# A two-layer hybrid attention step: first weights loaded earlier, squares moved to ScalarE, the softmax scale folded into the query copies

## Chip, cores and metric

The program runs on one core of one Trainium2 chip. The metric is the device time of one execution in microseconds. Before the change it is 833.89 us, the median of three runs (833.1 to 834.7).

## What is computed

Two trunk layers act on 512 latent and 128 context tokens (640 columns) of width 1024, in fp32. A layer computes

```python
mod = silu(cond) @ ada_w + ada_b             # shift, scale, gate: 3 x 1024, for c and for c_ctx
h = rmsnorm(x, norm_g) * (1 + scale) + shift
parts = h @ w_in                             # width 3872, cut into ten parts
# A: latent attention, 4 heads, softmax(q k / sqrt(96)) v
# B: gated convolution of width 3
# C: differential attention, 4 heads: softmax(q0 k0 / 8) - lam * softmax(q1 k1 / 8), times v, then a norm
x = x + gate * ((concat(A, B, C) * silu(z)) @ w_out)
```

Latent queries see the latent keys and 128 cached context keys, context queries only the 128 context keys. Outputs are the final norm of x and the context states.

## The kernel before

Activations lie transposed: 128 channels on the partitions, 640 tokens along the free dimension, eight such tiles `hs[kt]` for the 1024 channels. Everything is handled in two halves `j` of 320 tokens. TensorE works in a split form: each fp32 operand becomes a rounded high part (a cast on ScalarE, L324, L390) and a low rest (a subtraction on VectorE, L326, L394; GpSimd does it for some weights), and a product is three matmuls (L362 to L364). Weights come in 15 units per layer of 256 or 272 columns, each in two halves of four `kt`, loaded on the SP queue (L319).

**The start.** The modulation of layer 0 needs `silu(cond) @ ada_w` for shift and scale. That is four blocks `cc` of eight 256 KB loads: blocks 2 and 3 make the scale, 0 and 1 the shift, each for one half of the channels. Block 0 is summed on VectorE (L448, L450), the others by fp32 matmuls on TensorE (L462), two instructions per load. A block's result goes through a copy on ScalarE (L465) and four small transposes (L468) into `mod`. SP's order is: blocks 2, 0, the first token half of x, block 3, the eight loads of block 1, unit `qk0`, the second token half of x, unit `dv0`. In program order eight block-1 products stand before the first projection `p0qk` (L969). The second half's squares for the norm run on GpSimd (L238) and are summed on VectorE (L245).

**The layer.** `main()` is a generator that yields after a few matmuls; `units()` yields one attention unit at a time (4 diff heads of 5 units, then 4 latent heads of 5). `adv` (L1043) mixes them: each advance runs one piece of `main`, steps the background pieces (weight casts, rotary, norms), and at fixed advance numbers (`SIDE0`, `C1`, `C2`, `SIDES`, L1050) one step of `side()`. A side step loads one 256 KB tile of the remaining modulation weights (L148) and reduces it twice on VectorE (L153). Layer 0 has 48 side steps, layer 1 has 16, for the gate that the output projection multiplies with (L1164). Counting the yields, a layer has 228 advances; layer 1 does its 16 steps at advances 24 to 92.

**A diff unit** (L599) makes two score tiles of 128x640 in PSUM (two buffers, shared with the transposes of the weights E). For each VectorE takes the row maximum (L624), then both are multiplied by the negative scale (L625), ScalarE takes the exponent with that bias and accumulates the sum (L631), VectorE makes the ratio (L633, L634) and combines both maps (L636). A latent unit does the same for one map (L886, L887, L889).

The instructions are put in order per engine by a scheduler at build time; an engine then works through its list in order. `pin` keeps an instruction behind what was traced before it on its engine.

Of the kernel before, what the change touches and what calls it, by code (L numbers as in the profile page):

```python
# [14 lines left out]
AF = mybir.ActivationFunctionType  # L15
ALU = mybir.AluOpType
# [3 lines left out]
P = 128  # L20
# [40 lines left out]
def tile_kernel(ctx: ExitStack, tc: tile.TileContext, i: dict, o: dict):  # L61
# [12 lines left out]
    PU = ("qk2", "cq1", "c01", "c11")  # L74
    QD, QM, SIDE0 = 5, 3, 18
    C1, C2 = 44, 126
    SIDES = (8, 4, 5)

# [261 lines left out]
    def unit(n, k=1, only_load=False, halves=2):  # L340
# [11 lines left out]
        return res  # L352

    def wtile(n, kt, cs):

        hi, lo = unit(n, 0 if n == 0 and kt < 4 else 1)[kt // 4]
        return hi[:, kt % 4, cs], lo[:, kt % 4, cs]
# [53 lines left out]
    x_dram = dr.tile([P, KT, T], F32, name="x_dram")  # L411
    norms = [Norm(0, "n0", "v", G), Norm(1, "n0", sq=G)]

# [41 lines left out]
    def ada_block(cc):  # L455
        pa, pt = pas[cc], pts[:, 8 * cc:8 * cc + 8]
        if cc == 0:
            for c in range(2):
                TE.matmul(pa[0:2, :], ec[:, c, :], aacc[cc, c], start=c == 0, stop=c == 1)
        else:  # L460
            for kt in range(KT):
                TE.matmul(pa[0:2, :], sc[:, kt, :], araw.pop((cc, kt)), start=kt == 0, stop=kt == KT - 1)  # L462
                yield
        rows = slot("rows%d" % cc, shape=(2, 512))
        S.copy(rows, pa[0:2, :])  # L465
        yield
        for k in range(4):
            TE.transpose(pt[:, k * 2:k * 2 + 2], rows[:, k * P:(k + 1) * P], ident[0:2, 0:2])  # L468
        ks = slice((cc % 2) * 4, (cc % 2) * 4 + 4)
        V.tensor_copy(mod[0][cc // 2][:, ks, :].rearrange("p k c -> p (k c)"), pt[:, 0:8])  # L470
        ada_fin(0, cc // 2, ks)
# [13 lines left out]
    next(rg)  # L485
    ada_mm(3, 2, 8)
    load_start(*[1] * 8)
    unit(0, 0, True, 1)
    ada_mm(1, 0, 2)
    rbs = [now(rg), None]  # L490
    next(ab[3])
    next(ab[0])
    now(ab[3])
    ts = {}
    for kt in range(KT):
        ts[kt] = scaled(0, 0, kt, rbs[0], xs)
    unit(0, 0, True, 2)
    ada_mm(1, 2, 4)
    now(ab[0])
    unit(0, 0)  # L500
    for kt in range(4):
        modulate(0, 0, kt, rbs[0], xs, hs, kt == 3, ts[kt])
    ada_mm(1, 4, 9)
    now(ab[1])
    for kt in range(KT):
# [5 lines left out]
    for l in range(DEPTH):  # L511
# [13 lines left out]

        def proj_raw(nm, b, js=(0, 1), r=None):
            r = r or slot("raw%d%s%d" % (l, nm, b))
            for j in js:
                ps = yield from proj(nm, b, j)
                S.copy(r[:, j * HB:(j + 1) * HB], ps)  # L530
                yield
            return r
# [47 lines left out]
        def qk_head(h):  # L580
            nm = "qk%d" % h
            res = r["qk%d" % h] = {}
            res["qr"] = q = yield from proj_raw(nm, 0)
            bg.append(q_post(h, q, res))
            res["kr"] = k = yield from proj_raw(nm, 1)
            bg.append(k_post(h, k, res))
# [12 lines left out]
        def diff_unit(h, u, qkh, vt, acc):  # L599
# [8 lines left out]
            if u < 4:  # L608
                for a in range(2):
                    ps = bank2("S%d" % a + tg).rearrange("p (j c) -> p j c", j=2)  # L610
                    qc = slice(u * 128, u * 128 + 128)
                    for j in range(2):
                        js = slice(j * HB, (j + 1) * HB)
                        TE.matmul(ps[:, j, 0:HB], qs[:, a, qc], kh[:, a, js], start=True, stop=False)  # L614
                        TE.matmul(ps[:, j, 0:HB], qs[:, a, qc], kl[:, a, js], start=False, stop=True)  # L615
                    Sv.append(ps[:, :, 0:HB])
            else:
                ps = bank2("S" + tg)
                for a in range(2):
                    own = slice(a * 64, a * 64 + 64)  # L620
                    TE.matmul(ps[:, a * 512:a * 512 + 128], ctxv(q)[own], ctxv(k)[own], start=True, stop=True)
                    Sv.append(ps[:, a * 512:a * 512 + 128])
            for a in range(2):
                V.tensor_reduce(out=sm[:, a:a + 1], in_=Sv[a], axis=AX.XY if u < 4 else AX.X, op=ALU.max)  # L624
            V.tensor_scalar(out=sm[:, 2:4], in0=sm[:, 0:2], scalar1=-DIFF_SCALE, scalar2=None, op0=ALU.mult)  # L625
            E = []
            for a in range(2):
                e = slot("E%d" % a + tg)
                ev = e if u < 4 else e[:, 0:128]
                so = s0[:, u:u + 1] if a == 0 else sm[:, 5:6]  # L630
                S.activation(ev, Sv[a], AF.Exp, bias=sm[:, 2 + a:3 + a], scale=DIFF_SCALE, accum_out=so)  # L631
                E.append(e)
            V.reciprocal(sm[:, 6:7], sm[:, 5:6])  # L633
            V.tensor_scalar(out=sm[:, 7:8], in0=s0[:, u:u + 1], scalar1=sm[:, 6:7], scalar2=neglam[:, l:l + 1],  # L634
                            op0=ALU.mult, op1=ALU.mult)
            V.scalar_tensor_tensor(out=E[0][:, 0:nk], in0=E[1][:, 0:nk], scalar=sm[:, 7:8], in1=E[0][:, 0:nk],  # L636
# [137 lines left out]
        def q_norm(cq):  # L774
# [24 lines left out]
            for m in (2, 0, 1):  # L799
                for j in range(2):  # L800
# [5 lines left out]
                    yield  # L806
                    S.copy(qp[m][:, js], ps)
                if m == 2:
# [60 lines left out]
        def mla_unit(h, u, qq, kk, kc, get_vm, os_, pairs):  # L869
# [13 lines left out]
            else:  # L883
                TE.matmul(ps[:, 0:128], ctxv(qm), kc[:, h, :], start=True, stop=True)
                Sv = ps[:, 0:128]
            V.tensor_reduce(out=sm[:, 0:1], in_=Sv, axis=AX.XY if u < 4 else AX.X, op=ALU.max)  # L886
            V.tensor_scalar(out=sm[:, 1:2], in0=sm[:, 0:1], scalar1=-MLA_SCALE, scalar2=None, op0=ALU.mult)  # L887
            e = slot("E" + tg)
            S.activation(e if u < 4 else e[:, 0:128], Sv, AF.Exp, bias=sm[:, 1:2], scale=MLA_SCALE,  # L889
                         accum_out=sm[:, 2:3])  # L890
# [65 lines left out]
        def main():  # L956
# [4 lines left out]
            for j in range(2):  # L961
                ps = [bank("p%dqk0%d%d" % (l, b, j))[:, 0:HB] for b in range(2)]
                js = slice(j * HB, (j + 1) * HB)
                for kt in range(KT):
                    for k in (0, 1) if kt == 0 else (kt + 1,):
                        if k < KT and (j == 1 or l == 0 and k >= 4):
                            modulate(l, j, k, rbs[j], xs, hs, k == KT - 1, ts.get(k) if j == 0 else None)
# [9 lines left out]
                    if l == 0 and j == 0:  # L977
                        if kt == 1:
                            for k in range(KT):
                                norms[1].add(xs[k], k)  # L980
                        if kt == 6:
                            rg = norms[1].rstd()
                            next(rg)
                    yield
                for b in range(2):
                    S.copy(raws[b][:, js], ps[b])
                if j == 0:
# [55 lines left out]
        def adv(n):  # L1043
            for _ in range(n):
# [4 lines left out]
                cnt[0] += 1  # L1049
                if cnt[0] > SIDE0 and cnt[0] % SIDES[0 if cnt[0] < C1 else 1 if cnt[0] < C2 else 2] == 0:  # L1050
                    next(sg, None)
# [86 lines left out]
        while "gate" not in r:  # L1138
            next(sg)

# [175 lines left out]
```

## Time and profile before

| | before |
|---|---|
| median of runs | 833.89 us |
| profiled execution, its own time | 832.23 us |
| its span | 830.2 us |
| PE busy | 783.8 us (94%) |
| DVE busy | 633.4 us (76%) |
| ACT busy | 445.8 us (54%) |
| POOL busy | 70.0 us (8%) |
| mean granted clock | 0.992 |
| shares of the chain that ended last | PE 60%, DVE 18%, ACT 9%, DMA 7% |

The span is the profiled part; 2.0 us of the execution's own time lie around it. PE is the matmul engine, DVE VectorE, ACT ScalarE, POOL GpSimd, SP the queue that issues loads. A bracket such as [0.67 <-ACT hh L390] means that the engine stood idle for 0.67 us before the row and what released it.

### The profile page before, as it was taken

Reading aid. Unit: us, or ns where it says so; the run is one execution under the profiler, and the core shown is the slowest. Engines: PE = TensorE matmul, PEld = TensorE weight load, DVE = VectorE, ACT = ScalarE, POOL = GpSimd, SP = SyncE. Lnnn points to the kernel's source line nnn. Section 1 sums busy time; section 2 is a strip of 40 time slices with the busy share of each in tenths; the row PEclk is TensorE's granted clock in tenths of the full one; section 3 lists DMA queues with packets and bytes.
Section 4 is the critical chain, followed back from the end, with each engine's and each line's share of the span. In section 5 each row is a group of like instructions: output and inputs, shape, how many; then the busy total and the mean of one; then the engine's idle time right before and its main releaser. Section 6 shows DMA issues by size and latency. Waiting matters only on the chain.

```text
span 830.2 us, 14320 instructions
## 1 busy us (share of the span) xinstructions
PE 783.8 (94%) x5390; PEld 739.3 (89%) x5390; DVE 633.4 (76%) x1494; ACT 445.8 (54%) x978; POOL 70.0 (8%) x45
## 2 busy tenths in 40 slices
PE   6999999989999899999999999999999899999994
PEld 1389988989999888999999998899999899899994
DVE  4788989989998778789567778987778556668535
ACT  2255447454747667674334545546557667756310
POOL 3300011030001102000220002003000200200000
PEclk9999999999999999999999999999999999999997
DMA  8916434132420322135620433411111001111503
GB/s 311 386 66 197 131 104 135 44 92 71 157 83 27 107 90 83 45 120 184 240 102 22 154 103 109 143 30 58 51 59 52 26 26 52 51 53 50 179 1 126
DMA packets 66164, 85.52 MB, mean 103 GB/s; under 512 B 4976, under 2 KB 47408, under 8 KB 66096
## 3 DMA queue, kind: packets, MB, share of 16 engines
q1 hardware_dynamic: 65520, 83.96, 30.9%
q8 instruction: 42, 0.69, 0.3%
q10 hardware_dynamic: 576, 0.66, 0.2%
q14 instruction: 26, 0.21, 0.1%
HBM read 78.14 MB, written 6.46 MB: 102 GB/s over the span
## 4 chain that ended last, share of the span: by engine, by line
PE 60%; DVE 18%; ACT 9%; DMA 7%; issue 3%; POOL 1%; SPq 1%; POOLq 0%; DVEq 0%; ACTq 0%
PE wo L363 5%; PE wo L362 4%; PE wo L364 4%; DVE jk L153 4%; DVE sm L624 2%; ACT E L631 2%; PE O L645 2%; PE p1c L362 2%; PE p1c L364 2%; PE p1c L363 2%; PE tpm L900 2%; PE p1qk L363 2%; PE p1qk L362 2%; PE S L614 2%; PE p1qk L364 2%
## 5 line engine op out<-in xcount | busy, mean ns | idle before, releaser
L153 DVE CUSTOM_DVE_ANT_0 jk<-at,cb 128x512 bf16<-128x512 f32 x128 | 91.9, 718 | 4.9 <-DMA at<-in_adaT 4.2
L631 ACT ACTIVATE E<-S,sm 128x640 f32<-128x640 f32 (+1 forms) x80 | 56.0, 706 | 61.4 <-DVE sm L625 43.3
L363 PE MATMUL wo<-mx,who 128*128 128x320 f32 x256 | 79.3, 311 | 0.1
L364 PE MATMUL wo<-mx,wlo 128*128 128x320 f32 x256 | 79.0, 309 | 0.0
L362 PE MATMUL wo<-mx,who 128*128 128x320 f32 x256 | 78.5, 310 | 0.0
L624 DVE TENSOR_REDUCE sm<-S 128x1 f32<-128x640 f32 (+1 forms) x80 | 55.3, 711 | 3.4 <-PE S L615 2.4
L889 ACT ACTIVATE Em<-Sm,smm 128x640 f32<-128x640 f32 (+1 forms) x40 | 28.3, 708 | 41.9 <-DVE smm L887 40.5
L236 ACT ACTIVATE sqn<-xn 128x320 f32<-128x320 f32 x32 | 15.1, 471 | 64.8 <-DVE xn L1164 64.5
L363 PEld LDWEIGHTS wo<-mx,who 128*128 128x128 f32 x256 | 48.1, 188 | 0.8 <-DVE mx L274 0.6
L614 PE MATMUL S<-kh,qs 128*128 128x320 f32 x128 | 40.7, 327 | 8.5 <-ACT E L631 8.4
L364 PEld LDWEIGHTS wo<-mx,wlo 128*128 128x128 f32 x256 | 48.1, 188 | 0.0
L362 PEld LDWEIGHTS wo<-mx,who 128*128 128x128 f32 x256 | 47.8, 188 | 0.0
L362 PE MATMUL v<-whi_dv,hh 128*128 128x272 f32 x160 | 46.3, 289 | 0.0
L363 PE MATMUL v<-wli_dv,hh 128*128 128x272 f32 x160 | 46.0, 288 | 0.0
L364 PE MATMUL v<-whi_dv,hl 128*128 128x272 f32 x160 | 46.0, 288 | 0.0
L645 PE MATMUL O<-v,atd 128*128 128x128 f32 x336 | 44.1, 275 | 0.2 <-ACT atd L596 0.2
L1164 DVE SCALAR_TENSOR_TENSOR xn<-wo,mod,xn 128x320 f32<-128x320 f32 (+2 forms) x48 | 19.6, 435 | 31.2 <-PE wo L364 21.4
L645 PEld LDWEIGHTS O<-v,atd 128*128 128x128 f32 x336 | 42.1, 192 | 0.5 <-ACT atd L596 0.5
L363 PE MATMUL p0qk<-hl,whi_qk 128*128 128x320 f32 x128 | 40.2, 315 | 2.4 <-DVE hl L394 2.4
L326 POOL TENSOR_TENSOR wli_c<-ri_c,whi_c 128x1024 fp32r<-128x1024 f32 x8 | 19.8, 2475 | 264.7 <-PE p0zm L363 85.4
L362 PE MATMUL p1c<-hh,whi_c 128*128 128x320 f32 x128 | 41.6, 325 | 0.0
L362 PE MATMUL p0c<-hh,whi_c 128*128 128x320 f32 x128 | 41.2, 322 | 0.0
(377 smaller groups left out, 2660.6 us busy)
## 6 DMA issues: line engine op xcount, KB each, us to landing
at<-in_adaT SPq DMA_DIRECT2D x64, 256.0 KB, 4.0
ada<-in_adaA SPq DMA_DIRECT2D x32, 256.0 KB, 5.1
ri_qk<-in_wi SPq DMA_DIRECT2D x16, 512.0 KB, 4.8
ri_c<-in_wi SPq DMA_DIRECT2D x16, 512.0 KB, 4.0
ro<-in_wo SPq DMA_DIRECT2D x16, 512.0 KB, 4.4
ri_dv<-in_wi SPq DMA_DIRECT2D x8, 544.0 KB, 4.6
ri_zd<-in_wi SPq DMA_DIRECT2D x8, 512.0 KB, 3.7
x<-in_xT SPq DMA_DIRECT2D x16, 160.0 KB, 4.8
```

What stands on the lines that cost most here:

```text
L153: V.tensor_tensor_reduce(out=junk, in0=raw, in1=cb2[:, c, :], scale=1.0, scalar=0.0, op0=ALU.mult, op1=ALU.add, accum_out=acc)
L326: eng.tensor_tensor(out=lo, in0=raws[hf], in1=hi.bitcast(F32), op=ALU.subtract)
L362: TE.matmul(ps, ah, bh, start=first, stop=False)
L363: TE.matmul(ps, ah, bl, start=False, stop=False)
L364: TE.matmul(ps, al, bh, start=False, stop=last)
L614: TE.matmul(ps[:, j, 0:HB], qs[:, a, qc], kh[:, a, js], start=True, stop=False)
L624: V.tensor_reduce(out=sm[:, a:a + 1], in_=Sv[a], axis=AX.XY if u < 4 else AX.X, op=ALU.max)
L631: S.activation(ev, Sv[a], AF.Exp, bias=sm[:, 2 + a:3 + a], scale=DIFF_SCALE, accum_out=so)
L645: TE.matmul(po[:, 0:128], at[:, c * 128:(c + 1) * 128], vv[:, h * 128:(h + 1) * 128], start=c == 0, stop=c == n - 1)
L889: S.activation(e if u < 4 else e[:, 0:128], Sv, AF.Exp, bias=sm[:, 1:2], scale=MLA_SCALE, accum_out=sm[:, 2:3])
L900: TE.transpose(tp[:, c * 128:(c + 1) * 128], toktile(e, c), ident)
L1164: V.scalar_tensor_tensor(out=xn[kt][:, a:e], in0=ps[:, a - j * HB:e - j * HB], scalar=mod[l][2][:, kt, c:c + 1], in1=xn[kt][:, a:e], op0=A ...
```

## The change

Six edits go together.

1. SP issues the first half of unit `qk0` before block 1's eight loads, the second half after them. `unit_half` lets the first four `kt` start when only the first half is split.
2. Of block 1's eight products four stay ahead of the first projection, two come after its first `kt` and two after its second; block 1's transposes and sums come at `kt` 3. Block products and transposes on TensorE are pinned. Scaling and modulating `kt` 0 to 3 are interleaved.
3. The second token half's squares go to ScalarE, two at a time from `kt` 4 on; the norm's sums over partitions follow at `kt` 7 in place of 6.
4. The copies of the queries out of PSUM multiply by the negative scale (-1/8, or -1/sqrt(96)). The row maximum becomes a row minimum that is the bias itself, the exponent has scale -1, and the multiplications L625 and L887 go.
5. The ratio L634 becomes a scalar_tensor_tensor.
6. The side steps have a table for each layer. Layer 0 keeps its steps but for one at advance 44. Layer 1 has none until advance 50, and then one at each multiple of 12: 60, 72, up to 228, that is 15, and the sixteenth after the last advance.

```diff
-    SIDES = (8, 4, 5)
+    SIDES = (((18, None), (44, 8), (126, 4), (9999, 5)), ((50, None), (9999, 12)))
...
+    def unit_half(hf):
+        g, res = loaded[0]
+        while len(res) <= hf:
+            next(g)
+        return res
...
-        hi, lo = unit(n, 0 if n == 0 and kt < 4 else 1)[kt // 4]
+        hi, lo = (unit_half(0) if n == 0 and kt < 4 else unit(n))[kt // 4]
...
-    norms = [Norm(0, "n0", "v", G), Norm(1, "n0", sq=G)]
+    norms = [Norm(0, "n0", "v", G), Norm(1, "n0")]
...
-                TE.matmul(pa[0:2, :], sc[:, kt, :], araw.pop((cc, kt)), start=kt == 0, stop=kt == KT - 1)
+                pin(TE.matmul(pa[0:2, :], sc[:, kt, :], araw.pop((cc, kt)), start=kt == 0, stop=kt == KT - 1))
...
-            TE.transpose(pt[:, k * 2:k * 2 + 2], rows[:, k * P:(k + 1) * P], ident[0:2, 0:2])
+            pin(TE.transpose(pt[:, k * 2:k * 2 + 2], rows[:, k * P:(k + 1) * P], ident[0:2, 0:2]))
...
+    unit(0, 0, True, 1)
     load_start(*[1] * 8)
-    unit(0, 0, True, 1)
-    ada_mm(1, 0, 2)
+    next(ab[3])
     rbs = [now(rg), None]
-    next(ab[3])
     next(ab[0])
+    unit(0, 0, True, 2)
+    next(loaded[0][0])
     now(ab[3])
+    now(ab[0])
     ts = {}
-    for kt in range(KT):
+    ts[0] = scaled(0, 0, 0, rbs[0], xs)
+    unit_half(0)
+    modulate(0, 0, 0, rbs[0], xs, hs, False, ts[0])
+    for kt in range(1, 4):
         ts[kt] = scaled(0, 0, kt, rbs[0], xs)
-    unit(0, 0, True, 2)
-    ada_mm(1, 2, 4)
-    now(ab[0])
-    unit(0, 0)
-    for kt in range(4):
         modulate(0, 0, kt, rbs[0], xs, hs, kt == 3, ts[kt])
-    ada_mm(1, 4, 9)
-    now(ab[1])
+    ada_mm(1, 0, 4)
+    for kt in range(4, KT):
+        ts[kt] = scaled(0, 0, kt, rbs[0], xs)
...
+                    if l == 0 and j == 0 and kt == 3:
+                        unit_half(1)
+                        now(ab[1])
...
-                        if kt == 1:
-                            for k in range(KT):
+                        if kt < 2:
+                            ada_mm(1, 4 + 2 * kt, 6 + 3 * kt)
+                        if kt >= 4:
+                            for k in (2 * kt - 8, 2 * kt - 7):
                                 norms[1].add(xs[k], k)
-                        if kt == 6:
+                        if kt == KT - 1:
...
-            res["qr"] = q = yield from proj_raw(nm, 0)
+            res["qr"] = q = yield from proj_raw(nm, 0, -DIFF_SCALE)
...
-                V.tensor_reduce(out=sm[:, a:a + 1], in_=Sv[a], axis=AX.XY if u < 4 else AX.X, op=ALU.max)
-            V.tensor_scalar(out=sm[:, 2:4], in0=sm[:, 0:2], scalar1=-DIFF_SCALE, scalar2=None, op0=ALU.mult)
+                V.tensor_reduce(out=sm[:, a:a + 1], in_=Sv[a], axis=AX.XY if u < 4 else AX.X, op=ALU.min)
...
-                S.activation(ev, Sv[a], AF.Exp, bias=sm[:, 2 + a:3 + a], scale=DIFF_SCALE, accum_out=so)
+                S.activation(ev, Sv[a], AF.Exp, bias=sm[:, a:a + 1], scale=-1.0, accum_out=so)
...
-            V.tensor_scalar(out=sm[:, 7:8], in0=s0[:, u:u + 1], scalar1=sm[:, 6:7], scalar2=neglam[:, l:l + 1],
-                            op0=ALU.mult, op1=ALU.mult)
+            V.scalar_tensor_tensor(out=sm[:, 7:8], in0=s0[:, u:u + 1], scalar=sm[:, 6:7], in1=neglam[:, l:l + 1],
+                                   op0=ALU.mult, op1=ALU.mult)
...
-                    S.copy(qp[m][:, js], ps)
+                    copy(qp[m][:, js], ps, -MLA_SCALE)
...
-                if cnt[0] > SIDE0 and cnt[0] % SIDES[0 if cnt[0] < C1 else 1 if cnt[0] < C2 else 2] == 0:
+                every = next(n for end, n in SIDES[l] if cnt[0] <= end)
+                if every and cnt[0] % every == 0:
                     next(sg, None)
```

`copy(dst, src, scale)` is `S.copy` without a scale and an `S.activation` of `Copy` with one. The latent unit's L886 to L889 change as the diff unit's do.

## Rows read from the trace of the kernel before

**Rows 1.** The page: busy us, share of the span, instructions of each engine.

```profile
PE 783.8 (94%) x5390; PEld 739.3 (89%) x5390; DVE 633.4 (76%) x1494; ACT 445.8 (54%) x978; POOL 70.0 (8%) x45
```

**Rows 2.** Waits of PE over the whole run: total us, times, longest.

```profile
PE S L614 <- ACT E L631: 8.4, 6, 3.1
PE tpd L594 <- ACT E L631: 4.7, 4, 2.1
...
PE p0qk L363 <- DVE hl L394: 2.4, 4, 0.9
...
PE Sm L362 <- DVE smm L887: 1.9, 2, 1.2
PE p0qk L362 <- ACT hh L390: 1.4, 2, 0.8
```

**Rows 3.** PE's timeline at the first projection: start us, us, what, idle before.

```profile
33.41 3.60 PE L462 MATMUL pa<-ada,sc 128*2 128x512 f32 x8
37.67 0.56 PE L362 MATMUL p0qk<-hh,whi_qk 128*128 128x320 f32 x2 [0.67 <-ACT hh L390]
```

**Rows 4.** Timelines of SP and ACT: loads of modulation blocks, first weight cast.

```profile
13.29 12.15 SPq L441 DMA_DIRECT2D ada<-in_adaA  x20
...
31.91 1.04 ACT L324 CAST whi_qk<-ri_qk 128x1024 fp32r<-128x1024 f32 x1 [0.31 <-DMA ri_qk<-in_wi]
```

**Rows 5.** Timelines of POOL, DVE and ACT at the start: squares, low parts.

```profile
33.94 8.50 POOL L238 TENSOR_TENSOR sqn<-x 128x320 f32<-128x320 f32 x8 [13.43 <-DMA x<-in_xT]
...
38.08 3.78 DVE L394 SCALAR_TENSOR_TENSOR hl<-t,mod,hh 128x320 fp32r<-128x320 f32 x4
...
45.95 0.55 DVE L394 SCALAR_TENSOR_TENSOR hl<-t,mod,hh 128x320 fp32r<-128x320 f32 x1
...
8.04 0.47 ACT L236 ACTIVATE sqn<-x 128x320 f32<-128x320 f32 x1 [5.35 <-DMA x<-in_xT]
```

**Rows 6.** Groups of DVE instructions: count, busy us, mean ns, idle before.

```profile
L153 DVE CUSTOM_DVE_ANT_0 jk<-at,cb 128x512 bf16<-128x512 f32 x128 | 91.9, 718 | 4.9 <-DMA at<-in_adaT 4.2
...
L634 DVE TENSOR_SCALAR sm<-s,sm,neglam 128x1 f32<-128x1 f32 x40 | 10.9, 272 | 1.0
...
L625 DVE TENSOR_SCALAR sm<-sm 128x2 f32<-128x2 f32 x40 | 7.6, 189 | 0.4
...
L887 DVE TENSOR_SCALAR smm<-smm 128x1 f32<-128x1 f32 x40 | 6.0, 150 | 0.7
```

**Rows 7.** Timelines of POOL, DVE and PE around 500 us (layer 1, diff units).

```profile
497.19 2.79 POOL L326 TENSOR_TENSOR wli_qk<-ri_qk,whi_qk 128x1024 fp32r<-128x1024 f32 x1 [67.94 <-PE p1qk L363]
...
497.75 2.78 DVE L153 CUSTOM_DVE_ANT_0 jk<-at,cb 128x512 bf16<-128x512 f32 x1
...
500.46 1.54 DVE L624 TENSOR_REDUCE sm<-S 128x1 f32<-128x640 f32 x2
...
502.76 0.17 DVE L625 TENSOR_SCALAR sm<-sm 128x2 f32<-128x2 f32 x1
...
503.90 0.76 PE L594 MATMUL tpd<-idw,E 128*128 128x128 f32 x5 [2.06 <-ACT E L631]
```

**Rows 8.** Timelines of DVE and PE around 176 us (layer 0).

```profile
174.98 1.11 DVE L625 TENSOR_SCALAR sm<-sm 128x2 f32<-128x2 f32 x1
...
176.99 0.41 PE L614 MATMUL S<-kh,qs 128*128 128x320 f32 x1 [3.11 <-ACT E L631]
```

**Rows 9.** Stretches: length, busy us (instructions) of PE, PEld, DVE, ACT, POOL; clock.

```profile
520.00:530.00 10.00, 8.00 (x47) 7.71 (x46) 9.38 (x27) 5.50 (x15) 0.00 (x0) 0.83 0.28 85
530.00:540.00 10.00, 10.00 (x73) 9.97 (x73) 8.96 (x27) 5.28 (x14) 0.00 (x0) 1.00 0.58 194
```

**Rows 10.** Two stretches of layer 1: length, busy us of DVE, clock.

```profile
485.00:557.00 72.00, 64.54 (x149) 0.98 0.29 91
557.00:757.00 200.00, 136.44 (x313) 1.00 0.15 46
```

**Rows 11.** SP's timeline in layer 1: eight weight loads.

```profile
604.22 83.78 SPq L319 DMA_DIRECT2D ri_c<-in_wi  x8
```

More of the change, by code (lines that the diff above doesn't have):

```diff
@@ L74, in tile_kernel @@
     PU = ("qk2", "cq1", "c01", "c11")
-    QD, QM, SIDE0 = 5, 3, 18
-    C1, C2 = 44, 126
-    SIDES = (8, 4, 5)
+    QD, QM = 5, 3
+    SIDES = (((18, None), (44, 8), (126, 4), (9999, 5)), ((50, None), (9999, 12)))
     def slot(name, dt=F32, shape=(P, T)):
@@ L524, in proj, with copy, proj_raw @@
             return ps
-        def proj_raw(nm, b, js=(0, 1), r=None):
-            r = r or slot("raw%d%s%d" % (l, nm, b))
-            for j in js:
+        def copy(dst, src, scale=None):
+            if scale is None:
+                S.copy(dst, src)
+            else:
+                S.activation(dst, src, AF.Copy, scale=scale)
+        def proj_raw(nm, b, scale=None):
+            r = slot("raw%d%s%d" % (l, nm, b))
+            for j in range(2):
                 ps = yield from proj(nm, b, j)
-                S.copy(r[:, j * HB:(j + 1) * HB], ps)
+                copy(r[:, j * HB:(j + 1) * HB], ps, scale)
                 yield
@@ L885, in mla_unit @@
                 Sv = ps[:, 0:128]
-            V.tensor_reduce(out=sm[:, 0:1], in_=Sv, axis=AX.XY if u < 4 else AX.X, op=ALU.max)
-            V.tensor_scalar(out=sm[:, 1:2], in0=sm[:, 0:1], scalar1=-MLA_SCALE, scalar2=None, op0=ALU.mult)
+            V.tensor_reduce(out=sm[:, 0:1], in_=Sv, axis=AX.XY if u < 4 else AX.X, op=ALU.min)
             e = slot("E" + tg)
-            S.activation(e if u < 4 else e[:, 0:128], Sv, AF.Exp, bias=sm[:, 1:2], scale=MLA_SCALE,
+            S.activation(e if u < 4 else e[:, 0:128], Sv, AF.Exp, bias=sm[:, 0:1], scale=-1.0,
                          accum_out=sm[:, 2:3])
@@ L985, in main @@
                 for b in range(2):
-                    S.copy(raws[b][:, js], ps[b])
+                    copy(raws[b][:, js], ps[b], -DIFF_SCALE if b == 0 else None)
                 if j == 0:
@@ L1138, in tile_kernel @@
         while "gate" not in r:
-            next(sg)
+            next(sg, None)
         while bg:
```

## The prediction

> **What bounds the kernel now.** The page comes first: TensorE is busy 783.8 of 830.2 us [rows 1], so no other engine's work costs time by itself. What can be won is TensorE's idle time, 46 us, and the little that it runs at the lower clock. The second view is therefore TensorE's waits by what ended them [rows 2]. The largest are the diff units' waits for the exponent: score matmuls wait 8.4 us for a PSUM buffer that the exponent still reads, transposes 4.7 us for the weights that it makes, ten waits with 13.1 us in all. The latent units' scores wait 1.9 us behind L887 in two waits. The first projection waits 2.4 us for low parts and 1.4 us for high parts, 3.8 us in six waits. The third view is the timeline around such a wait, because the releaser named is only the last link. Before the wait of 2.06 us at 503.90, VectorE stood in a side reduction from 497.75 to 500.46; it then took both row maxima until 502.0, ran another instruction, and multiplied by the scale only at 502.76 [rows 7]. Before the wait of 3.11 us at 176.99 the scale multiplication itself took 1.11 us in place of its mean of 0.19 [rows 6, 8]. So the softmax chain is late where VectorE's list is full. Last come the stretches: VectorE is busy 64.5 of 72 us while layer 1 does its side steps, and 136 of the 200 us after that [rows 10].
>
> **The start (edits 1 to 3).** SP issues twenty modulation loads in 12.15 us, 0.61 us each [rows 4]. Eight of them now stand behind the first weight half, which is issued 8 x 0.61 = 4.9 us sooner. Its cast began at 31.91, 0.31 us after ScalarE ran dry and as soon as the load had landed [rows 4]; it can now begin some 4.9 us earlier, as far as ScalarE's block copies allow, which is no longer what the projection waits for. On TensorE nothing is removed: the eight block-1 products stay; four of them, eight instructions, cost 3.60 us [rows 3], and four now follow the first and second `kt`. The first projection matmul stood at 37.67 after 0.67 us of idle time [rows 3]; without that idle time and with 3.60 us of products behind it, it comes at about 33.4. The work moved is a filler: it lies where the projection waited for `kt` 0 to 3. What goes is hence at most the 3.8 us of waits [rows 2]. Two new waits stand against it. Block 0's transposes are pinned and need its copy, so TensorE stands about half a microsecond between them and the four block-1 products; and block 1's sums now come at `kt` 3, so `kt` 4 waits for an add, a high part and a low part, about 0.5 us more. What stands behind them on TensorE is delayed by either.
>
> The squares take GpSimd 8.50 us [rows 5]. On ScalarE they cost 8 x 0.47 = 3.8 us [rows 5], beside an engine that is busy 54% [rows 1]. VectorE gains: four low parts took 3.78 us while GpSimd squared, 0.95 each, and one took 0.55 us afterwards [rows 5], so 4 x 0.4 = 1.6 us of its list in the very stretch where TensorE waits for low parts. If that cover were missing, the squares would be late for the norm of the second half, whose values the `v` matmuls hide now.
>
> Bounds of this part: -3.8 us if all six waits go, +1.0 us if the loads land no sooner and both new waits count. I take -2.8, the first end less the two new waits of 0.5, as the low-part rows speak for it.
>
> **The softmax scale (edits 4, 5).** VectorE loses 40 x 0.189 = 7.6 us and 40 x 0.150 = 6.0 us [rows 6]. The ratio costs 0.272 us as a tensor_scalar with two column scalars; the nearest row with one is L625 with 0.189 [rows 6], so 0 to 0.08 us each, 0 to 3.3 us, and I take 3. The scaled copies and the minimum do not show in the trace; the nearest are the plain copy and the maximum, which do the same number of elements, and I take no difference, with 40 x 0.1 = 4 us of VectorE's and ScalarE's work either way as bounds, hidden or not like the rest. These 17 us of VectorE's 633 lie beside TensorE's work and give nothing directly. What counts is the chain between maximum and exponent. At 500 us it was 502.93 - 502.00 = 0.93 us long [rows 7], at 176 us more than 1.11 us [rows 8], and at its shortest it is the instruction itself, 0.19 us [rows 6]. Besides, the first map's exponent needs only its own minimum now and can start while VectorE takes the second (1.54 us for two [rows 7], so 0.77 us sooner). I take 0.9 us for each of the ten diff waits, 9 us, and 0.4 us for both latent waits, 0.8 us. What is late next is the exponent itself and the side work in VectorE's list, and the scheduler lays every list anew. So I count half: -4.9 us. Bounds: 0, and -13.1 - 1.9 = -15.0 if all these waits go [rows 2].
>
> **The side steps (edit 6).** Layer 1's sixteen steps stood at advances 24 to 92, that is up to 557 us. Three (60, 72, 84) stay there, and thirteen move on. Each is 2 x 0.718 = 1.4 us of VectorE [rows 6], so 19 us leave the stretch in which VectorE was busy 90%, and come to one in which it was busy 68% [rows 10]. At 497.75 a side reduction took 2.78 us in place of 0.72, beside a GpSimd subtraction of 2.79 us [rows 6, 7]; without it the row maxima begin at 497.8 and TensorE's wait of 2.06 us has no cause. In 520 to 530 TensorE issued 47 matmuls against 73 in the next ten microseconds [rows 9]: 26 x 10/73 = 3.6 us lost, 2.0 of them idle and the rest at a granted clock of 0.83 on average, so some of it at 1.2 in place of 2.4 GHz. Both together are 5.6 us, of which 2 x 0.9 = 1.8 are counted above; 3.8 remain, and I take half, -1.9 us, for the reason that follows. In the later stretch 13 x 1.4 = 19 us are spread over 200 us; bounds are 0, if they fall into VectorE's idle third, and +5 us, if a quarter of it delays a score. I take +1.2, near the first, as VectorE is idle 64 us there [rows 10]. The sixteenth step comes after the last advance; its result is wanted at the first L1164, some 3.3 us later by the 24 matmuls of 10/73 us before it, with PSUM buffers for three more such groups. Cover enough for a load, and without that cover the load's few microseconds would be paid.
>
> Why only half: the row at 497.75 shows GpSimd and VectorE in each other's way. The Trainium skill, "SBUF — State Buffer", section "Who interferes with whom", says that the two share a pair of ports as an exclusive lock, and that a VectorE instruction with two SBUF inputs is blocked wholly by a GpSimd instruction that reads SBUF. By that rule the GpSimd subtraction stays and holds up whichever such instruction is next in VectorE's list; the term would be the clock part alone, about -0.8, and the whole sum -7.4. The trace agrees as far as the 2.78 us go; no row here shows what stands in that place after the change.
>
> **Sum.** -2.8 - 4.9 - 1.9 + 1.2 = -8.4 us. The profiled execution's own time is 832.23, which gives 823.8; it is 1.7 us under the median of the runs, 833.89, which gives 825.5. I predict 825.5 us.
>
> **Rivals.**
> 1. *The waits go nearly in full*: -3.8 at the start, -11 of the 15.0 us of softmax waits, -3 at the side steps is -17.8, so 816 us. For it: the chain shortens in every one of eighty places, and a wait that is gone also spares clock. Against it: a wait in a full list is moved as often as it is removed.
> 2. *The waits change place*: VectorE's list stays above 90% busy in the diff units of both layers, the exponents are early, and TensorE waits for the transposes' copies and for low weight parts in place of them. Only the start's idle time of 1 us or so is kept: 833 us. For it: the diff stretch has VectorE at 90% [rows 10]. Against: the change takes 17 us off that list. This is also the case in which the change doesn't do what it says, as the loads land no sooner.
> 3. *Slower, by side loads that come late in layer 1*: the side loads now share SP's list with the last weight loads, of which eight stretched over 83.8 us [rows 11], so each of them waited for a buffer some ten microseconds. A side load behind such a one lands late, VectorE stands at its reduction (it did so for 4.2 us in the whole run before [rows 6]), and row minima queue behind it. Seven or eight steps lie there; if four stall by 3 us each more than TensorE has other work for, that is +12, with the rest of the sum +3.6: 837.5 us. It decides from about 8.4 us of such stalls. For it: 83.8 us for eight loads. Against: layer 0 does the same at every fourth and fifth advance, and all its stalls are in the 4.2 us.
>
> **How the numbers follow.** Forecast 0.64 (821 to 831), rival 1 0.12, rival 2 0.13, rival 3 0.11. A change of 0.2%, 1.7 us, is about what can be told from none, so "same" is 832.2 to 835.6. Faster: the forecast, rival 1 and a sixth of rival 2, 0.64 + 0.12 + 0.02 = 0.78. Same: most of rival 2, 0.10. Slower: rival 3 and a little of rival 2, 0.12. The range must leave out no more than 0.2: 818 to 834 leaves out rival 3 and half of rival 1.
>
> **What would show it.** At the start: the first projection matmul at 33 to 34.5 us with waits on it below 1.5 us, low parts of 0.5 us throughout, no GpSimd squares after 33 us. In the softmax: no L625 and L887, exponents that start 0.1 us after a minimum, and less than 8 us in the two waits for the diff exponent. In layer 1: 26 more matmuls in the ten microseconds about 520, a clock of 1.00 there, side reductions up to 757 us. I am wrong if the projection starts before 35 and the second half's norm is no earlier (step 1), if the diff waits stay at 13 us with the multiplications gone (step 2), or if VectorE's idle time for side loads grows past 8 us (step 3).

## The result and the profile after

The changed kernel takes 826.81 us (median of four runs, 824.56 to 828.43) beside 834.3 us for the kernel before on the same chip (833.1 to 836.36): ratio 0.9889, 95% interval 0.9852 to 0.9925. The forecast was 825.5. The quotient of the two medians, 0.9910, is not the ratio, though it lies in its interval: the gain is 7.5 us by the medians and 9.3 by the ratio, and every difference against the changed kernel below is uncertain by some 2 us for that alone. The profiled execution of after is the slowest of its four (828.43), that of before (832.23) is faster than any of its four, so the two traces differ by 3.8 us only; sizes below are ratios, and the traces serve to find places.

The page of after, and TensorE's waits by what ended them (total us, times, longest), beside [rows 1, 2]:

```profile
PE 786.2 (95%) x5390; PEld 742.7 (90%) x5390; DVE 619.1 (75%) x1414; ACT 453.3 (55%) x986; POOL 60.5 (7%) x37
```

```profile
PE S L630 <- ACT E L647: 4.9, 3, 3.6
...
PE st_n L212 <- DVE sqn L245: 4.6, 2, 2.6
PE Sm L369 <- ACT Em L904: 3.7, 4, 1.6
...
PE p0qk L370 <- DVE hl L401: 2.2, 3, 1.0
```

VectorE lost 14 us and 80 instructions. The waits for the diff exponent fell from 13.1 us to 5.5 (4.9 here, 0.6 in the transposes' row). Two rows grew above all: the latent scores' wait for the exponent, 3.7 us where before had 0.6 (and 1.9 behind the multiplication that is gone), and the wait of the norm sums for squares, 2.6 us at the longest where before had 1.9.

The longest of these, 2.61 us, belongs to the start. Timelines of after for PE, ACT and DVE:

```profile
33.85 0.41 PE L369 MATMUL p0qk<-hh,whi_qk 128*128 128x320 f32 x1
...
46.52 0.41 PE L370 MATMUL p0qk<-hl,whi_qk 128*128 128x320 f32 x1 [1.04 <-DVE hl L401]
50.86 1.24 PE L212 MATMUL st_n<-ones,sqn 128*128 128x1 f32 x6 [2.61 <-DVE sqn L245]
51.96 0.57 PE L369 MATMUL v<-whi_dv,hh 128*128 128x272 f32 x1
```

```profile
29.84 1.04 ACT L324 CAST whi_qk<-ri_qk 128x1024 fp32r<-128x1024 f32 x1
...
39.73 0.58 ACT L472 COPY rows<-pa 2x512 f32<-2x512 f32 x1 [4.90 <-PE pa L469]
...
42.47 0.81 ACT L236 ACTIVATE sqn<-x 128x320 f32<-128x320 f32 x2
...
47.53 0.82 ACT L236 ACTIVATE sqn<-x 128x320 f32<-128x320 f32 x2
...
72.09 0.44 ACT L540 ACTIVATE raw0qk<-p0qk 128x320 f32<-128x320 f32 x1 [1.64 <-PE p0qk L371]
```

```profile
41.14 0.17 DVE L477 COPY mod<-pts 128x8 f32<-128x8 f32 x1 [3.89 <-PE pts L475]
...
48.43 1.28 DVE L326 TENSOR_TENSOR wli_dv<-ri_dv,whi_dv 128x1088 fp32r<-128x1088 f32 x1
49.63 1.08 DVE L245 TENSOR_TENSOR sqn<-sqn,sqn 128x320 f32<-128x320 f32 x2
...
58.55 1.25 DVE L380 SCALAR_TENSOR_TENSOR t<-x,mod,rb_n 128x192 f32<-128x192 f32 x4 [4.67 <-PE rb_n L220]
```

The same two places in before, PE and ACT:

```profile
47.55 0.72 PE L212 MATMUL st_n<-ones,sqn 128*128 128x1 f32 x6
```

```profile
67.07 0.86 ACT L986 COPY raw0qk<-p0qk 128x320 f32<-128x320 f32 x2 [1.65 <-PE p0qk L364]
```

The first projection begins at 33.85 (37.67 before, [rows 3]). But ScalarE stands idle for 4.90 us before 39.73 and takes its eight squares only between 42.47 and 48.3, in among casts and high parts. VectorE adds the last of them at 49.63, after a weight subtraction of 1.28 us that stands ahead of it in its list; TensorE's norm sums wait 2.61 us for that, and in the next stretch its granted clock is 0.66 where before had 1.00 (length, busy us of PE, PEld, DVE, ACT, POOL, clock; before first, then after):

```profile
50.00:60.00 10.00, 10.00 (x78) 10.00 (x77) 7.47 (x29) 6.67 (x16) 0.00 (x0) 1.00 0.13 50
```

```profile
50.00:60.00 10.00, 9.14 (x49) 9.17 (x50) 3.52 (x16) 2.24 (x6) 0.00 (x0) 0.66 0.02 7
```

The query copy of the second half comes at 72.09, in before at 67.07. So the start ends 5.0 us later than before.

Around 500 us the picture of [rows 7, 9, 10] is gone. POOL, DVE and PE, then three stretches:

```profile
498.86 5.20 POOL L326 TENSOR_TENSOR wli_qk<-ri_qk,whi_qk 128x1024 fp32r<-128x1024 f32 x2 [67.94 <-PE p1qk L370]
```

```profile
498.97 2.85 DVE L572 TENSOR_TENSOR qs<-raw1qk,qs 64x512 fp32r<-64x512 f32 x1
502.04 2.03 DVE L650 SCALAR_TENSOR_TENSOR sm<-s,sm,neglam 128x1 f32<-128x1 f32 x1
```

```profile
518.90 0.41 PE L630 MATMUL S<-kh,qs 128*128 128x320 f32 x1 [0.97 <-ACT E L647]
```

```profile
520.00:530.00 10.00, 9.80 (x70) 9.76 (x70) 8.92 (x22) 6.05 (x15) 0.00 (x0) 1.00 0.40 133
...
485.00:557.00 72.00, 70.84 (x508) 69.70 (x506) 57.18 (x112) 44.77 (x106) 5.12 (x2) 1.00 0.21 68
557.00:757.00 200.00, 195.23 (x1386) 189.66 (x1386) 147.50 (x327) 130.43 (x286) 16.10 (x9) 1.00 0.21 64
```

GpSimd's two subtractions still hold one VectorE instruction each: a rotary product takes 2.85 us (0.69 elsewhere), and the one-column ratio, 0.22 us as a rule, takes 2.03. But neither stands between a minimum and its exponent, so TensorE's longest wait from 485 to 557 us is 0.97 us, 70 matmuls were issued in 520 to 530 in place of 47, and the clock is 1.00.

### The profile page after: what moved, and what is told of

Its sections match the earlier page's. It is cut to its first block, busy times and chain, and to the rows that moved or that the text cites. A ratio compares the mean times of both kernels' runs of the same rounds, so it can differ in the third digit from the quotient of the medians.

```text
span 826.7 us, 14182 instructions
## 1 busy us (share of the span) xinstructions
PE 786.2 (95%) x5390; PEld 742.7 (90%) x5390; DVE 619.1 (75%) x1414; ACT 453.3 (55%) x986; POOL 60.5 (7%) x37
## 4 chain that ended last, share of the span: by engine, by line
PE 70%; DVE 13%; DMA 6%; ACT 6%; issue 3%; POOL 1%; SPq 1%; POOLq 0%; DVEq 0%; ACTq 0%
PE wo L370 4%; PE wo L371 4%; PE wo L369 4%; PE O L661 3%; DVE jk L153 2%; PE v L369 2%; PE v L371 2%; PE v L370 2%; PE S L630 2%; PE p1qk L370 2%; PE p1qk L369 2%; PE p1qk L371 2%; PE p1c L370 2%; PE p1c L369 2%; PE p1c L371 2%
## 5 line engine op out<-in xcount | busy, mean ns | idle before, releaser
L153 DVE CUSTOM_DVE_ANT_0 jk<-at,cb 128x512 bf16<-128x512 f32 x128 | 89.6, 700 | 8.8 <-DMA at<-in_adaT 7.5
L369 PE MATMUL v<-whi_dv,hh 128*128 128x272 f32 x160 | 47.4, 296 | 0.0
L371 PE MATMUL v<-whi_dv,hl 128*128 128x272 f32 x160 | 47.1, 295 | 0.0
L370 PE MATMUL v<-wli_dv,hh 128*128 128x272 f32 x160 | 47.1, 294 | 0.0
L369 PE MATMUL p1qk<-hh,whi_qk 128*128 128x320 f32 x128 | 40.4, 317 | 0.0
L369 PE MATMUL p0qk<-hh,whi_qk 128*128 128x320 f32 x128 | 40.0, 322 | 0.0
```

The costliest lines, as they stand in the source:

```text
L153: V.tensor_tensor_reduce(out=junk, in0=raw, in1=cb2[:, c, :], scale=1.0, scalar=0.0, op0=ALU.mult, op1=ALU.add, accum_out=acc)
L369: TE.matmul(ps, ah, bh, start=first, stop=False)
L370: TE.matmul(ps, ah, bl, start=False, stop=False)
L371: TE.matmul(ps, al, bh, start=False, stop=last)
```

## The experiments

All ratios are against the kernel before on the same chip, five rounds each; "us" behind one is the ratio less 1, times 834 us.

**The three parts alone.** start_only has edits 1 to 3, softmax_only 4 and 5, side_only 6. The edit of side_only is the whole of edit 6:

```diff
-    SIDES = (8, 4, 5)
+    SIDES = (((18, None), (44, 8), (126, 4), (9999, 5)), ((50, None), (9999, 12)))
...
```

> The kernel before with edits 1 to 3 alone (start and squares). Theory A, from the two traces: the second-half norm is late because its squares are given to ScalarE only from kt 4 on, TensorE stands 2.6 us and then runs at 1.2 GHz for some 6 us; the copy of the second half of the first projection, at 67.1 us before, comes at 72 us, and nothing later makes up for it: 839 us (+5). Rival B: the stages behind have slack that absorbs it, 834 us. The forecast's step said -2.8, 831.5 us.

Measured 839.76 us, ratio 1.0032 (1.0003 to 1.0060), +2.7 us. The start's part is a loss by itself, between theory A's +5 and rival B's nothing.

> The kernel before with edits 4 and 5 alone. Theory A: since the start lost 5 us and the whole won 7.5, folding the scale is worth more than the forecast's 4.9: about -9, so 825 us, with the two waits for the diff exponent (13.1 us before) under 7 us. Rival B: the start lost nothing in the end and the fold is worth -4.9: 829.4 us. Rival C: the gain is the side steps', and the fold alone gives under 2 us: 832.5 us or more.

Measured 831.43 us, ratio 0.9941 (0.9913 to 0.9969), -4.9 us. That is the predicted term to the tenth, with an interval of 2.3 us to each side; theory A's -9 lies outside it. The two diff waits fell from 13.1 to 8.8 us, not under 7.

> The kernel before with edit 6 alone (side steps of layer 1 spread out). The forecast's terms: -1.9 + 1.2 = -0.7, 833.6 us. Theory A: -3, 831 us, with the stretch about 520 us at full clock. Rival: the steps only change place, 834.3 us. Of the slower rival: 836 us or more, with more than 8 us of VectorE's waits for side loads.

Measured 836.81 us, ratio 1.0003 (0.9976 to 1.0030), +0.3 us: no change that can be told. VectorE's waits for side loads are 5.5 us here, so it is not rival 3 that ate the gain.

The parts sum to -1.9 us, the whole is -9.3. So the terms don't add.

**Each part left out.** no_start is edits 4 to 6 with the start of before, no_side edits 1 to 5, no_soft edits 1 to 3 and 6. The edit of no_side, against the changed kernel:

```diff
-    SIDES = (((18, None), (44, 8), (126, 4), (9999, 5)), ((50, None), (9999, 12)))
+    SIDES = (((18, None), (43, 8), (125, 4), (9999, 5)), ((18, None), (43, 8), (125, 4), (9999, 5)))
```

> Edits 4 to 6 on the kernel before (its own start). Theory A, the scale and the side steps are two causes of the same waits of layer 1, so that only both together free them, and the start costs about 2.7 us everywhere: the whole (ratio 0.989) without the start's loss, ratio 0.985 to 0.987, about 11 to 12 us under the kernel before; layer 1 from its first p1zd to its first p1ckq takes 47 us (51.4 before). Theory B, the parts add up and the whole's gain is an accident of one order: ratio 0.994 (-4.9 + 0.6 us), that stretch 50 us or more.

Measured 826.11 us, ratio 0.9890 (0.9867 to 0.9914), -9.2 us.

> The changed kernel with the side steps where they were (edits 1 to 5). Theory A: the fold alone keeps its 4.9 us and the start loses 2.7: ratio 0.997, and layer 1's stretch from p1zd to p1ckq stays at 51 us. Rival, the side steps matter as little as they did alone: the ratio stays at 0.989 and the stretch at 47 us.

Measured 834.88 us, ratio 1.0001 (0.9982 to 1.0019).

> The changed kernel with the multiplications by the scale put back and the old ratio (edits 1 to 3 and 6). Theory A: start +2.7, side steps +0.7: ratio 1.003 to 1.005, the stretch of layer 1 at 50 to 51 us. Rival, the start and the side steps carry the whole's gain together and the fold nothing: ratio 0.989.

Measured 841.55 us, ratio 1.0079 (1.0051 to 1.0107), +6.6 us.

The fold and the side steps together give 9.2 us, where the two alone sum to 4.6, as theory A's two causes would have it. But theory A expected 0.985 to 0.987, as its start was to cost 2.7 us everywhere, and no_side and no_soft came out slower than it said (0.997; 1.003 to 1.005). The fold is worth 4.9 us alone and 15.9 in company (1.0079 less 0.9889), the side steps 0.3 loss alone and 9.3 gain in company; the intervals make each of the two figures in company uncertain by some 4 us. Stages of the profiled executions, each from the first matmul of one group to that of the next (p0 and p1 are projections of layer 0 and 1, wo layer 0's output projection), worked out from the first start of each (us, one execution each; the last six kernels come further down):

| kernel | to p0zd | to p0zm | to wo | to p1zd | to p1ckq | to the end | span |
|---|---|---|---|---|---|---|---|
| before | 108.7 | 131.1 | 133.9 | 125.1 | 51.4 | 280.0 | 830.2 |
| after | 112.5 | 129.6 | 134.4 | 124.0 | 47.1 | 279.1 | 826.7 |
| start_only | 113.6 | 133.8 | 134.3 | 125.2 | 51.4 | 280.3 | 838.6 |
| softmax_only | 108.3 | 129.3 | 138.7 | 124.1 | 51.6 | 277.7 | 829.7 |
| side_only | 108.8 | 132.2 | 136.5 | 124.9 | 49.8 | 282.2 | 834.4 |
| no_start | 107.9 | 128.2 | 135.2 | 123.7 | 47.2 | 279.8 | 822.0 |
| no_side | 112.7 | 130.7 | 138.2 | 124.2 | 52.0 | 278.5 | 836.3 |
| no_soft | 111.9 | 132.3 | 138.1 | 125.0 | 49.8 | 279.7 | 836.8 |
| early_squares | 105.7 | 128.5 | 136.3 | 123.9 | 47.2 | 281.2 | 822.8 |
| mult_kept | 111.8 | 131.7 | 139.2 | 126.5 | 50.0 | 281.5 | 840.7 |
| mult_beside | 110.7 | 129.8 | 134.1 | 124.0 | 47.4 | 280.3 | 826.2 |
| no_pool | 111.0 | 124.9 | 128.5 | 124.1 | 45.7 | 275.6 | 809.8 |
| no_side_no_pool | 110.6 | 125.2 | 128.9 | 124.1 | 49.7 | 274.8 | 813.3 |
| early_no_pool | 107.3 | 124.2 | 128.5 | 123.9 | 45.7 | 274.6 | 804.2 |

Two columns are plain. To p0zd, the changed kernel and the three partial ones with edits 1 to 3 are 3.1 to 4.9 us later than their twins without them. To p1ckq, fold and side steps together give 4.2 us (no_start), the fold alone nothing, the side steps alone 1.6. The column to wo is not: the four kernels with one of the two lose 2.6 to 4.8 us there, and no_start, with both, 1.3. So more of what doesn't add lies in layer 0 than in layer 1, though edit 6 takes only one side step out of layer 0. softmax_only shows where (POOL, DVE, PE):

```profile
319.39 5.31 POOL L326 TENSOR_TENSOR wli_c<-ri_c,whi_c 128x1024 fp32r<-128x1024 f32 x2 [49.90 <-PE p0c L363]
320.22 5.16 DVE L860 TENSOR_TENSOR kml<-krf,kmh 32x640 fp32r<-32x640 f32 x2
...
326.64 0.63 PE L362 MATMUL Sm<-kmh,qmh 96*128 96x320 f32 x1 [3.53 <-ACT Em L893]
```

Two VectorE instructions of 0.82 us as a rule stand beside two GpSimd subtractions for 5.16 us together; a row minimum queues behind them, and TensorE waits 3.53 us. The granted clock is 0.76 in 320 to 330 and 0.90 in the ten microseconds after. In the traces of the four kernels with one of the two edits, and in mult_kept further down, two of these instructions are held (136.5 to 139.2 us to wo); in before, after, start_only, no_start, early_squares and mult_beside one is (133.9 to 136.3). Which it is follows from how the scheduler laid the list; no run holds the list fixed, so why both edits together give the better list is not shown.

A like place is in no_side at 517 us, where it is a side reduction that is held; three more reductions and three other instructions run ahead of the first of the two minima behind it, a fourth reduction between the two (timelines of POOL, DVE, ACT, PE):

```profile
517.23 3.22 POOL L326 TENSOR_TENSOR wli_qk<-ri_qk,whi_qk 128x1024 fp32r<-128x1024 f32 x1 [10.30 <-ACT whi_qk L324]
...
518.52 2.48 DVE L153 CUSTOM_DVE_ANT_0 jk<-at,cb 128x512 bf16<-128x512 f32 x1
...
524.86 0.29 DVE L641 TENSOR_REDUCE sm<-S 128x1 f32<-128x128 f32 x1
...
526.00 0.37 ACT L647 ACTIVATE E<-S,sm 128x128 f32<-128x128 f32 x1 [2.50 <-DVE sm L641]
...
526.85 0.64 PE L630 MATMUL S<-kh,qs 128*128 128x320 f32 x1 [3.56 <-ACT E L647]
```

Two more of the kernels with one of the two edits have such places in layer 1: side_only (DVE, PE), where the scale's multiplication is held, and softmax_only (DVE, PE), where a side reduction is:

```profile
503.80 2.20 DVE L624 TENSOR_SCALAR sm<-sm 128x2 f32<-128x2 f32 x1
...
506.97 0.77 PE L593 MATMUL tpd<-idw,E 128*128 128x128 f32 x5 [2.40 <-ACT E L630]
```

```profile
512.54 2.49 DVE L153 CUSTOM_DVE_ANT_0 jk<-at,cb 128x512 bf16<-128x512 f32 x1
...
520.88 0.64 PE L620 MATMUL S<-kh,qs 128*128 128x320 f32 x1 [3.05 <-ACT E L636]
```

**The link or the work?** mult_kept puts a needless multiplication by 1.0 back between minimum and exponent; mult_beside has the same 80 instructions, but nobody reads them:

```diff
+            V.tensor_scalar(out=sm[:, 2:4], in0=sm[:, 0:2], scalar1=1.0, scalar2=None, op0=ALU.mult)
...
-                S.activation(ev, Sv[a], AF.Exp, bias=sm[:, a:a + 1], scale=-1.0, accum_out=so)
+                S.activation(ev, Sv[a], AF.Exp, bias=sm[:, 2 + a:3 + a], scale=-1.0, accum_out=so)
```

(mult_beside has the first line alone, the latent units likewise.)

> The changed kernel with one needless VectorE multiplication by 1.0 between the row minimum and the exponent, in all 80 units; the copies stay scaled. Theory A1, what the fold gives is the link it takes out of the chain from minimum to exponent: nearly all of what the fold gave is lost again, ratio 0.998 to 1.004, with the exponent waits of TensorE back at 10 us or more. Rival A2, the fold gives by another thing (the scaled copies, the ratio's new form, the order): the ratio stays within 0.3% of 0.989.

Measured 842.65 us, ratio 1.0084 (1.0052 to 1.0115), 16.3 us more than the change. That is beyond theory A1's range too (0.998 to 1.004); the waits for the diff exponent are back at 11.5 us.

> The changed kernel with the same 80 needless multiplications on VectorE as in mult_kept, at the same place, but the exponent reads the minimum and nobody reads the product. Theory A1, the fold's worth is the link in the chain from minimum to exponent: the ratio stays at 0.989 to 0.993. Rival A3, its worth is VectorE's time (14 us of instructions): the ratio goes to 0.998 or more, as with mult_kept (1.008).

Measured 827.85 us, ratio 0.9910 (0.9883 to 0.9937), 1.8 us more than the change, within the intervals.

So VectorE's time was worth nearly nothing and the link nearly all of it, together with the lists that the scheduler lays around it: 4.8 of the 14.0 us between the profiled executions of mult_kept and after lie in the column to wo, where two instructions are held in place of one. The two traces show the same instruction held by the same GpSimd subtraction, first mult_kept (DVE, ACT, PE), then mult_beside:

```profile
510.56 2.20 DVE L642 TENSOR_SCALAR sm<-sm 128x2 f32<-128x2 f32 x1
...
512.80 0.79 ACT L648 ACTIVATE E<-S,sm 128x640 f32<-128x640 f32 x1 [4.13 <-DVE sm L642]
...
513.74 0.77 PE L610 MATMUL tpd<-idw,E 128*128 128x128 f32 x5 [2.40 <-ACT E L648]
```

```profile
499.91 2.23 DVE L642 TENSOR_SCALAR sm<-sm 128x2 f32<-128x2 f32 x1
```

Where the exponent reads its result, ScalarE stands 4.13 us and TensorE 2.40; where nobody does, TensorE has no wait over 0.95 us from 495 to 560.

**The start: place of the squares.** early_squares is the changed kernel with the eight squares traced at the first `kt` and the norm's sums at `kt` 6:

```diff
+                        if kt == 0:
+                            for k in range(KT):
+                                norms[1].add(xs[k], k)
                         if kt < 2:
                             ada_mm(1, 4 + 2 * kt, 6 + 3 * kt)
-                        if kt >= 4:
-                            for k in (2 * kt - 8, 2 * kt - 7):
-                                norms[1].add(xs[k], k)
-                        if kt == KT - 1:
+                        if kt == 6:
```

> The changed kernel with the second half's squares traced at kt 0 in place of two at a time from kt 4, and the norm's sums at kt 6. Theory A: ScalarE and VectorE, idle from 35 to 40 us and from 37 to 41 us in the changed kernel, do the squares and sums there; TensorE's 2.6 us wait and the low clock behind it go, the copy comes at 66 to 67 us, and the time falls by 5 us against the changed kernel: 821.5 us. Rival B (what the start loses is absorbed later): 826 to 827 us.

Measured 823.81 us, ratio 0.9841 (0.9799 to 0.9883), 4.0 us under the changed kernel, with intervals that overlap. Its ACT and PE timelines and the stretch that was at 0.66:

```profile
34.37 3.00 ACT L236 ACTIVATE sqn<-x 128x320 f32<-128x320 f32 x7
```

```profile
42.37 0.80 PE L212 MATMUL st_n<-ones,sqn 128*128 128x1 f32 x6 [0.75 <-DVE mod L161]
```

```profile
50.00:60.00 10.00, 10.00 (x77) 9.90 (x76) 8.24 (x23) 6.17 (x15) 0.00 (x0) 1.00 0.01 2
```

Seven squares fill the gap in which ScalarE stood idle, the norm sums come 8.5 us earlier, and layer 0's stage to p0zd is 6.8 us shorter than in the changed kernel and 3.0 us shorter than before. Beside its twin without edits 1 to 3 (no_start, 107.9) the stage is 2.2 us shorter. So with the squares in the gap the start is worth, up to there, about what was forecast of it (2.8 us), and the place of the squares took more than that away: 6.8 us by this stage, of which 3.9 are left at the end of the span.

**Who makes the weights' low parts.** no_pool moves sixteen of GpSimd's subtractions to VectorE; early_no_pool does that in early_squares, no_side_no_pool in no_side:

```diff
-    PU = ("qk2", "cq1", "c01", "c11")
+    PU = ()
```

> The changed kernel with the sixteen weight subtractions that GpSimd makes inside the layers (qk2, cq1, c01, c11) on VectorE. Theory C, beside each of them one VectorE instruction stands for some 2 us, and which one it is decides on a TensorE wait and a stretch at the lower clock: the stretched VectorE instructions go at the attention units (19.3 us in the changed kernel, at most 9 here), VectorE takes 16 us of subtractions for them, and the ratio is 0.983 to 0.988. Rival, the subtractions on GpSimd relieve VectorE more than they hold it: VectorE's longer list delays the row minima, ratio 0.992 to 1.0.

Measured 811.80 us, ratio 0.9714 (0.9688 to 0.9740), -23.9 us.

> The same subtractions on VectorE, and layer 1's side steps where they were (edits 1 to 5). Theory C: with the collisions gone the side steps' place is worth far less than the 0.0112 between no_side (1.0001) and the changed kernel (0.9889): ratio within 0.004 of no_pool's. Rival, the side steps' own place in the busy stretch is what counts: 0.009 or more over no_pool's.

Measured 813.93 us, ratio 0.9733 (0.9708 to 0.9758).

> early_squares (squares traced at the first kt, ratio 0.9841) with the sixteen subtractions on VectorE. Theory C: both gains add up, ratio 0.978 to 0.983. Rival: VectorE's list becomes the limit, 0.985 or more.

Measured 806.32 us, ratio 0.9649 (0.9625 to 0.9674), -29.3 us: the fastest kernel here, faster than before and after.

Theory C holds; its ratios were too modest (0.983 to 0.988 for no_pool, 0.978 to 0.983 for early_no_pool). The list of after's waits has none for a low weight part, so low parts that come sooner don't explain it. The page of no_pool, and the rows of the subtractions on VectorE (busy us, mean ns), after first, then no_pool:

```profile
PE 781.2 (96%) x5390; PEld 739.8 (91%) x5390; DVE 614.7 (76%) x1430; ACT 452.1 (56%) x986; POOL 25.0 (3%) x21
```

```profile
L326 DVE TENSOR_TENSOR wli_c<-ri_c,whi_c 128x1024 fp32r<-128x1024 f32 x8 | 9.7, 1216 | 0.3 <-ACT Em L904 0.2
```

```profile
L326 DVE TENSOR_TENSOR wli_c<-ri_c,whi_c 128x1024 fp32r<-128x1024 f32 x16 | 19.5, 1217 | 1.4 <-PE p1zm L370 0.7 <-ACT whi_c L324 0.6
```

VectorE does sixteen instructions more, eight of them the 9.8 us in these two rows, and is busy 4.4 us less. The part of its instructions' time that lies over their group's median beside a GpSimd instruction (those with over 0.6 us of it, summed from the traces) was 17.9 us before, 21.1 after (the expectation has 19.3), and is 5.5 here; TensorE's idle time fell from 40.5 us to 28.6, its busy time by 5.0. The side steps' place is worth 0.0019 then, within the intervals, where it was 0.0112; by the stages it still gives 4.0 us up to p1ckq, where no_side_no_pool has a wait of 2.0 us for the exponent and no_pool none, and gives 0.8 back in the last stage.

## Why the prediction was right, step by step

The time was right (825.5 for 826.81; -8.4 us for -7.5 by the medians, -9.3 by the ratio), and of the three terms, each measured alone, only one was.

- **The start, -2.8 us: wrong**, in its sign, and at +2.7 past its bound of +1.0, which the interval (+0.2 to +5.0) doesn't exclude. By the text's own test (the second half's norm no earlier) it fell: the norm sums came at 50.86, in before's trace at 47.55. The earlier start came as forecast (33.85 for 33.4), the low parts took 0.54 us, none of the second half's squares was left on GpSimd, and the first projection's six waits of 3.8 us became three of 2.2. The step that failed is "On ScalarE they cost 8 x 0.47 = 3.8 us [rows 5], beside an engine that is busy 54% [rows 1]." The cost is right, the cover was an average: the squares are traced from `kt` 4 on and so lie behind the transposes and sums of block 1 that edit 2 put at `kt` 3. ScalarE was idle up to 39.73 and nearly full from there to 50.8. The cast came 2.1 us earlier (29.84 for 31.91, [rows 4]), not 4.9. The text named the price of a missing cover (late for the norm) and gave it no number: with it the part alone came to +2.7 us.
- **The softmax, -4.9 us: right in its mechanism, its size only alone.** Link and not work was the argument, and mult_kept and mult_beside show that: 16.3 us and 1.8. "So I count half" was exact for softmax_only (-4.9). In the whole, leaving the fold out costs 15.9 us, which can't be told from the bound of 15.0. That bound was the idle time in [rows 2] alone: of the 10.1 us between the profiled executions of no_soft and after, 3.9 are not idle time but a longer busy time of TensorE (790.1 for 786.2).
- **The side steps, -1.9 + 1.2 us: alone nothing, in company 9.3 us.** Its places were right: 70 matmuls in 520 to 530 for 47, clock 1.00, VectorE busy 57 us of 72 for 64.5 [rows 10]. VectorE's idle time for side loads grew from 4.2 us to 7.5, under the 8 at which rival 3 was to show; its price was not paid. The term of +1.2 is of the right size: in the last stage the five kernels with edit 6 that have a twin without it are between 0.6 us shorter and 2.2 longer than the twin. The term of -1.9 stands beside 1.6 us up to p1ckq alone and 4.4 to 4.9 with the fold. What the text put at nothing is layer 0: of the 9.6 us between the profiled executions of no_side and after, 3.8 lie in the stage to wo. (The recorded sum for a subtraction that stays is -7.3, not -7.4.)

```profile
L153 DVE CUSTOM_DVE_ANT_0 jk<-at,cb 128x512 bf16<-128x512 f32 x128 | 89.6, 700 | 8.8 <-DMA at<-in_adaT 7.5 <-DVE smm L906 0.3
```

- **The sum: right by two errors, which is luck.** Adding terms was itself the failed step: it takes the list around each edit for given. In layer 1 each of the traces shown has a VectorE instruction that stands for some 2 us beside a subtraction on GpSimd; which one, depends on what is next in the list. With the scale's multiplication there (mult_kept, side_only), or a side reduction (no_side, softmax_only), it lies ahead of an exponent and TensorE pays 2.4 to 3.6 us; with both gone it is a rotary product and the ratio, and TensorE pays 0.97. Each edit alone leaves the other's instruction in the place. That fits the column to p1ckq; in the larger one, to wo, it is the number of held instructions that differs, and why is open. The prediction had this row (2.78 us beside 2.79, [rows 7]) and used it to halve one term. By the Trainium skill ("SBUF — State Buffer", "Who interferes with whom") the subtraction holds whichever instruction comes next that needs the shared ports; the trace of after agrees (2.85 and 2.03 us). What the text didn't ask is what the whole kernel pays for that: no_pool says some 14.6 us (0.9889 less 0.9714).

Open is what the start costs in the whole. By the profiled stages it is 4.6 us there too; by the runs no_start and after are equal (0.9890 and 0.9889), with intervals of some 2 and 3 us to each side, and by the medians it is 1.5 us. early_squares against after (0.9841, 0.9889) overlaps as well; early_no_pool against no_pool (0.9649, 0.9714) does not, and gives 5.4 us for the squares' place.

## What to carry to other kernels

Edits that shorten one queue are not to be summed: ask for each which instruction will stand in the place of the one taken out, and whether a result that someone waits for comes behind it. Work that is moved to an engine "with room" needs a gap at the place where it is issued, not a low average. And an off-loaded instruction that holds another engine's instruction for its own length saves nothing: here sixteen subtractions on GpSimd made VectorE busier than doing them itself.

## What was not expected of the hardware

- A VectorE instruction of one or two columns can stand for about as long as a GpSimd subtraction: 0.17 us became 2.20 (L642 in mult_kept), 0.22 became 2.03 (L650 in after). Row minima and maxima from PSUM are in none of the traces among the instructions that were held by more than 0.6 us; five in before and three in after ran beside a GpSimd instruction and took 0.81 to 0.82 us, as elsewhere.
- After TensorE's wait of 2.61 us that ended at 50.86 the clock was 0.66 over 50 to 60; after the same wait of 2.62 us in no_pool it was 0.83 over that stretch; behind the 3.11 us at 176.99 in before [rows 8] it stayed at 1.00 from 170 to 190. The length of a wait alone doesn't give what the clock costs behind it.
